# A hybrid decoder layer in three-word fp32: Newton steps of three norms on VectorE one step behind, the first gate and up pair seeded in PSUM, residual loads moved back

## The chip, the cores and the metric

The kernel runs on one core of a Trainium2 chip. The metric is the device time of one execution in microseconds (us). The engines are called PE (TensorE, the matmuls), PEld (its weight loads), DVE (VectorE), ACT (ScalarE), POOL (GpSimd) and SP (SyncE, which here only issues DMAs).

## What is computed

One layer on 256 rows of 2048 channels, all in float32: a norm, one projection to queries, keys, values and gates, three kinds of causal attention over 16 heads, a branch projection for each kind with its sigmoid gate, an output projection with residual, a second norm, and a gated feed-forward of width 5632 with residual.

```python
h = rmsnorm(x, g_mix)
proj = h @ w_in                     # q, k, v (16 heads of 128) and 3 x 2048 gates
gates = sigmoid(proj[..., 3 * MIX_WIDTH:])
o_a = stick_breaking_attention(q[:4], k[:4], v[:4])
o_b = moba_attention(norm(q[4:10]), norm(k[4:10]), v[4:10], rel_bias)
o_c = dilated_attention(norm(q[10:]), norm(k[10:]), v[10:], rel_bias)
merged = (gates[0] * (flat(o_a) @ w_branch[:512]) + gates[1] * (flat(o_b) @ w_branch[512:1280])
          + gates[2] * (flat(o_c) @ w_branch[1280:]))
x = x + merged @ w_out
h2 = rmsnorm(x, g_ffn)
gu = h2 @ w_gu
return x + (silu(gu[..., :5632]) * gu[..., 5632:]) @ w_down
```

rmsnorm multiplies by the inverse root of the mean square of a row. The kernel applies that factor, `rstd`, only behind the matmuls, as the scale of the copy that takes a sum out of PSUM.

## The kernel before

**Products.** A weight tile of 128x1024 floats (`w_raw` or `g_raw`, 512 KB) is loaded by SP's queue and split on the fly into two words: ACT casts the high word (`w_hi`), DVE subtracts it and gets the low word (`w_lo`), both at line 110. `product` issues three matmuls: high by high (L181), low by high (L182), high by low (L183). Every weight tile thus costs one cast on ACT, one subtraction on DVE and usually twelve matmuls.

**Pairs.** `project_pair` computes two blocks of 512 columns at once. Over the channel chunks in `WC` it needs seven products instead of eight: some weight tiles are first added on DVE (tiles `u`, `g_raw` at L325 and L336), and the sums of the products (X and Y in the PSUM banks named `ps` or `qs`, Z and V in others) are put together afterwards. `form(ps, f, ...)` is one of the seven. In the plain way, snapshots of X and Z (L320) go to SBUF and are added back later on DVE (L390, L392, L406). With `seed=True` X is copied to Y and Z to V inside PSUM (L365, L367) and later products are summed on top. `begin_pair` does a pair's first loads and splits while the pair before still runs. There are two banks for each of the names `ps` and `qs`, so a new pair waits until the sums that were in its banks have been read.

**What goes beside the products.** Norms, attention, transposes and restored sums are written as generators in two queues, `stages` and `slow_stages`. At each split `advance` takes one step from `stages` (to the next `yield`), and at every other split one from `slow_stages`. How many yields stand between two pieces of work therefore sets how many splits apart they are. From the program so written a scheduler makes the order of each engine's queue. Each engine works through its queue in that order and never past an instruction that waits.

**The norms.** `rsqrt_mean` takes the mean, gets a first inverse root by Ln and Exp on ACT, and improves it with two Newton steps of four small operations each. It serves the first norm (`first_norm`, on POOL before the change), the norms of queries and keys (`rows_to_columns`) and `second_norm`, on DVE. `rstd` is needed by ACT's copy of the first values (`keep_v`, L781), by the gates (L767), and by `keep_qk` (L809, a DVE operation on tile `sst`). The first values are summed in two `ps` banks, the first gate in two `qs` banks; the first pair of queries and keys comes next and has X in the same `ps` banks.

**Attention.** `stick_breaking` masks its matrix `p` on POOL (L554) and yields three times before it multiplies by the values (L647). `softmax_pair` transposes (L203) and multiplies in the same manner.

**Second norm.** `next_h_now` turns the last two chunks of the second norm's input by transposes (chunks 2 and 3) while the first gate and up pair has begun; `second_norm` follows.

**Down projection.** `down_pair` runs twice, over 1024 columns each. In its loop over the plain weight tiles, `seven` supplies the seven products of each chunk in `WD`, with tiles `b11`, `b12`, `b22`, `b21`; the load of `b21` of the first such chunk is pinned in the queue (L107). `take_x1` loads the residual in four pieces of 256 KB (`sc<-x`, also L107), one at each step of the loop from i = 10 on. Meanwhile ACT still turns the last block of the hidden layer with two DMA transposes (L702).

Of the kernel before, what the change touches and what calls it, by code (L numbers as in the profile page):

```python
# [13 lines left out]
ALU = mybir.AluOpType  # L14
# [5 lines left out]
D = 2048  # L20
S = 256
NT = S // P
KT = D // P
HD = 128
# [3 lines left out]
D_FF = 5632  # L28
NF = D_FF // P
NB = 512  # L30
EPS = 1e-6
# [26 lines left out]
def hybrid_block(ctx: ExitStack, tc: tile.TileContext, x, rel_bias, w_in, w_branch, w_out, w_gu, w_down, xT, gains,  # L58
                 onehot, extra, out):
    nc = tc.nc  # L60
# [121 lines left out]
        nc.tensor.matmul(ps, ah, wl, start=False, stop=False, **how)  # L182
        nc.tensor.matmul(ps, al, wh, start=False, stop=stop, **how)  # L183

    def rsqrt_mean(dst, ss, n, cols, engine=nc.vector):

        v = small.tile([P, cols], F32, name=f"rs_v{cols}")
        engine.tensor_scalar(v, ss, 1.0 / n, EPS, op0=ALU.mult, op1=ALU.add)
        y = small.tile([P, cols], F32, name=f"rs_y{cols}")
        nc.scalar.activation(y, v, AF.Ln)  # L190
        nc.scalar.activation(y, y, AF.Exp, scale=-0.5)
        t = small.tile([P, cols], F32, name=f"rs_t{cols}")
        for it in range(2):
            engine.tensor_mul(t, y, y)
            engine.tensor_mul(t, t, v)
            engine.tensor_scalar(t, t, -0.5, 1.5, op0=ALU.mult, op1=ALU.add)
            engine.tensor_mul(dst if it else y, y, t)

    def transpose4(src):

# [236 lines left out]
    rstd = small.tile([P, NT], F32, name="rstd", bufs=1)  # L437
# [70 lines left out]
    def first_norm():  # L508
        for c in range(3, 4):
            squares(rows[c], ss1, c)  # L510
            yield
        sst = small.tile([P, NT], F32, name="sst", bufs=1)
        nc.vector.tensor_reduce(sst, ss1, op=ALU.add, axis=AX.X)
        rsqrt_mean(rstd, sst, D, NT, nc.gpsimd)
        yield

    rest = [rest_of_x()]
# [87 lines left out]
    def stick_breaking(hl, qT, kT, v):  # L605
        z = att.tile([P, 2 * NB], F32, name="att")
        for i in range(2):
            nc.tensor.matmul(z[:, i * S:(i + 1) * S], kT[:, hl + i, 0:P], qT[:, hl + i, :], start=True, stop=True)
        for i in range(2):
            nc.tensor.matmul(z[:, W0 + i * P:W0 + (i + 1) * P], kT[:, hl + i, P:S], qT[:, hl + i, P:S],  # L610
                             start=True, stop=True)
        n = W0 + W1
        l = pa.tile([P, n], F32, name="p", bufs=1)
        nc.scalar.activation(l, z[:, :n], AF.Abs)
        nc.scalar.activation(l, l, AF.Exp, scale=-1.0)
        nc.scalar.activation(l, l, AF.Ln, bias=1.0)
        sp = pa.tile([P, n], F32, name="pT", bufs=1)
        sp_hi = pa.tile([P, n], F32R, name="sp_hi", bufs=1)
        lo = half_kb(F32R), pa.tile([P, W1], F32R, name="sp_lo", bufs=1)
        nc.vector.scalar_tensor_tensor(sp, z[:, :n], 0.0, l, op0=ALU.max, op1=ALU.add)  # L620
        lb = l
        nc.vector.scalar_tensor_tensor(lb, z[:, :n], 0.0, l, op0=ALU.min, op1=ALU.subtract)
        for blk in diag_blocks(sp):
            keep_before(blk)
        nc.scalar.copy(sp_hi, sp)
        for part, cols in zip(lo, (slice(0, W0), slice(W0, n))):
            nc.vector.tensor_sub(part, sp[:, cols], sp_hi[:, cols].bitcast(F32))
        yield
        yield
        yield  # L630
        c = att.tile([P, 2 * NB], F32, name="att")
        late = c[:, 0:W0].rearrange("p (h q) -> p h q", h=2)[:, :, P:S]
        for i, (early, part) in enumerate(((sp_hi[:, 0:W0], sp_hi[:, W0:n]), lo)):
            nc.tensor.matmul(c[:, 0:W0], neg_after, early, start=not i, stop=False, skip_group_check=True)
            nc.tensor.matmul(late, neg_ones, part.rearrange("p (h q) -> p h q", h=2), start=False, stop=bool(i), skip_group_check=True)
            nc.tensor.matmul(c[:, W0:n], neg_after, part, start=not i, stop=bool(i), skip_group_check=True)
        nc.vector.tensor_add(lb, lb, c[:, :n])
        nc.scalar.activation(lb, lb, AF.Exp)
        for blk in diag_blocks(lb):
            keep_before(blk)  # L640
        yield
        yield
        yield
        po = tr.tile([P, 2, S], F32, name="tr")
        for i in range(2):
            cols = slice((hl + i) * HD, (hl + i + 1) * HD)
            nc.tensor.matmul(po[:, i, :], v[:, 0, cols], lb[:, i * S:(i + 1) * S], start=True, stop=False)  # L647
            nc.tensor.matmul(po[:, i, P:S], v[:, 1, cols], lb[:, W0 + i * P:W0 + (i + 1) * P],
                             start=False, stop=True)
        finish(hl, po)  # L650
# [61 lines left out]
    def rows_to_columns(g, sbs, dst):  # L712
        if g:
            ss = pa.tile([P, 4 * NT * 2], F32, name="ss", bufs=1)
            for i, sb in enumerate(sbs):
                junk = half_kb()
                for hd in range(4):
                    cols = slice(hd * HD, (hd + 1) * HD)
                    nc.scalar.activation(
                        junk[:, cols], sb[:, cols], AF.Square, accum_out=ss[:, 4 * i + hd:4 * i + hd + 1])  # L720
                yield
            rr = pa.tile([P, 4 * NT * 2], F32, name="rr", bufs=1)
            rsqrt_mean(rr, ss, HD, 4 * NT * 2)
            yield

        for i, sb in enumerate(sbs):
            if g:
                sb3 = sb.rearrange("p (h d) -> p h d", h=4)
                nc.vector.tensor_mul(sb3, sb3, rr[:, 4 * i:4 * i + 4, None].to_broadcast([P, 4, HD]))
                for _ in range(3):  # L730
                    yield
            j, t = divmod(i, NT)
            pt = transpose4(sb)
            d = dst[j][:, :, t * P:(t + 1) * P]
            if j == 0 and g:
                hs = 4 * g - H_A
                nc.vector.tensor_mul(d, backwards(pt), gq[:, hs:hs + 4, None].to_broadcast([P, 4, P]))
            else:
                nc.scalar.copy(d, pt)
            joined.append(j)  # L740
        yield
# [223 lines left out]
            behind(n + in_at[1] + 1, lambda: h2.put_sums(c, *[r[:, NB:].rearrange("p (k q) -> p k q", k=4) for r in rooms]))  # L965

    def next_h_now(c, xc):
        for _ in range(4 - c):
            yield
        for t in range(NT):  # L970
            pt = transpose4(xc[t])
            hs = half_kb().rearrange("p (k q) -> p k q", k=4)
            nc.vector.tensor_mul(hs, pt, g2[:, 4 * c:4 * c + 4, None].to_broadcast([P, 4, P]))
            h2.put(c, t, hs)
            yield
# [14 lines left out]
    for c in range(4):  # L990
# [13 lines left out]
            h2 = Chunks(pool(h2_stack, "h2p", "left"), "h", KT // 4, WC)  # L1004
            gx = pool(h2_stack, "gx2", "left", 2)
        if c == 3:
            ahead = begin_pair(h2, w_gu, 0, D_FF)
        keep_x1(c, ps, xc)
    pm.close()
    pr = pool(ctx, "pr", "right")  # L1010
# [3 lines left out]
    def second_norm():  # L1014
        sst2 = small.tile([P, NT], F32, name="sst2", bufs=1)
        nc.vector.tensor_reduce(sst2, ss2, op=ALU.add, axis=AX.X)
        rsqrt_mean(rstd2, sst2, D, NT)
        for _ in range(8):
            yield
        tc.keep_in_program_order(nc.scalar.preload_act_table_set("silu_and_others"))  # L1020
        yield
# [82 lines left out]
    def down_pair(c0, mine, spare, queues, more=(), pace=(6, 1)):  # L1104
# [85 lines left out]
        for i, at in enumerate(plain[:-4]):  # L1190
            rest(*at)
            if i >= 4 * len(more):
                next(with_sums, None)
            if i >= 10:
                next(x1_back, None)
            if i >= pace[0]:
                for _ in range(pace[1]):
# [52 lines left out]
```

## Time and profile before

| | |
|---|---|
| median of 3 runs | 1345.14 us (1344.11 to 1345.21) |
| profiled execution | 1351.32 us, span 1349.6 us |
| clock granted to PE, mean | 0.997 |
| PE, PEld busy | 1330.7 (99%), 1152.8 us (85%) |
| DVE, ACT, POOL busy | 1225.7 (91%), 943.3 (70%), 32.8 us (2%) |
| read from HBM | 292.13 MB, 226 GB/s over the span with the writes |

Everything that follows is read from one profiled execution, which is 6.2 us longer than the median of the runs that were timed. Of its 1351.32 us, 1.7 lie around the span. In the rows of the timeline the columns are the start, the duration, the engine, the line, the operation and its tiles; what stands in brackets is how long the engine sat idle before and which engine or load ended that. Durations of neighbours overlap, so what an operation takes in a full queue is the distance from its start to the next one's. By time, the program is: first values and gate to 49 us, queries, keys and attention to about 440, gates to 560, branches to 610, output projection to 690, eleven gate and up pairs to about 1130, and the two down pairs to the end.

### The profile page before, as it was taken

The page shows a single profiled execution, that of the slowest core. Times are in us where ns is not written, and L with a number is a line of the kernel's source. Part 1 is how long each engine was busy: PE and PEld are TensorE (multiplying, and loading weights), DVE is VectorE, ACT ScalarE, POOL GpSimd, SP SyncE. Part 2 cuts the span into 40 slices and gives each one's busy share as a digit, 9 for nine tenths or more (in the row PEclk, how much of TensorE's full clock was granted, in tenths as well). Part 3 has the DMA queues.
Part 4 walks back from the last instruction along what each step waited for, and adds up shares of the span by engine and source line. Part 5 has one row for each costly group of instructions (what it writes and reads, how often), then busy time and mean ns, then how long its engine had stood idle before and what let it go on. Part 6 is the DMA issues. An engine that isn't in the chain of part 4 may idle for free.

```text
span 1349.6 us, 17385 instructions
## 1 busy us (share of the span) xinstructions
PE 1330.7 (99%) x6194; PEld 1152.8 (85%) x6194; DVE 1225.7 (91%) x1294; ACT 943.3 (70%) x1209; POOL 32.8 (2%) x52
## 2 busy tenths in 40 slices
PE   9999999999999999999999999999999999899998
PEld 7788888888888888888878888888888888788887
DVE  6999999999999998784889999999999997899998
ACT  7777778688767666675757778787777786664663
POOL 0301100000000000000000000000000000000000
PEclk9999999999999999999999999999999999899999
DMA  9865556565666757999977767678887788978663
GB/s 342 285 237 171 174 191 226 189 203 171 238 225 239 241 181 227 292 280 221 267 249 246 243 206 243 206 218 262 261 244 256 212 278 222 309 252 276 221 223 103
DMA packets 200407, 314.79 MB, mean 233 GB/s; under 512 B 46424, under 2 KB 58224, under 8 KB 200320
## 3 DMA queue, kind: packets, MB, share of 16 engines
q1 hardware_dynamic: 151632, 291.54, 65.3%
q10 hardware_dynamic: 46800, 16.29, 6.4%
q0 software_dynamic: 1888, 5.86, 1.1%
q8 instruction: 48, 0.79, 0.2%
q14 instruction: 39, 0.32, 0.1%
HBM read 292.13 MB, written 12.60 MB: 226 GB/s over the span
## 4 chain that ended last, share of the span: by engine, by line
PE 43%; DMA 3%; DVE 2%; ACT 1%; issue 1%; SPq 0%; ACTq 0%; DVEq 0%
PE ps L181 4%; PE ps L183 4%; PE ps L182 4%; PE qs L182 4%; PE qs L183 4%; PE qs L181 4%; PE z L181 3%; PE z L182 3%; PE z L183 3%; PE v L181 2%; PE v L183 2%; PE v L182 2%; DVE w_lo L110 1%; PE tr L182 1%; PE tr L183 1%; PE tr L181 1%
## 5 line engine op out<-in xcount | busy, mean ns | idle before, releaser
L110 DVE TENSOR_TENSOR w_lo<-w_raw,w_hi 128x1024 fp32r<-128x1024 f32 x308 | 375.3, 1223 | 69.5 <-ACT w_hi L110 68.5
L110 ACT CAST w_hi<-w_raw 128x1024 fp32r<-128x1024 f32 x308 | 319.7, 1046 | 74.7 <-PE qs L183 18.6
L110 ACT CAST w_hi<-u 128x1024 fp32r<-128x1024 f32 x156 | 162.9, 1048 | 158.7 <-DVE u L325 87.1
L110 ACT CAST w_hi<-g_raw 128x1024 fp32r<-128x1024 f32 x208 | 213.4, 1048 | 75.6 <-DVE g_raw L325 27.4
L110 DVE TENSOR_TENSOR w_lo<-g_raw,w_hi 128x1024 fp32r<-128x1024 f32 x208 | 248.2, 1224 | 7.0 <-ACT w_hi L110 5.5
L110 DVE TENSOR_TENSOR w_lo<-u,w_hi 128x1024 fp32r<-128x1024 f32 x156 | 186.6, 1225 | 11.6 <-ACT w_hi L110 11.1
L182 PE MATMUL ps<-w_lo,h_hi 128*128 128x512 f32 x328 | 125.3, 382 | 1.7 <-DVE w_lo L110 1.6
L183 PE MATMUL ps<-w_hi,h_lo 128*128 128x512 f32 x328 | 124.3, 379 | 0.0
L182 PE MATMUL qs<-w_lo,h_hi 128*128 128x512 f32 x316 | 120.8, 382 | 0.0
L183 PE MATMUL qs<-w_hi,h_lo 128*128 128x512 f32 x316 | 119.9, 379 | 0.0
L181 PE MATMUL ps<-w_hi,h_hi 128*128 128x512 f32 x328 | 117.3, 380 | 0.0
L181 PE MATMUL qs<-w_hi,h_hi 128*128 128x512 f32 x316 | 112.4, 381 | 0.0
L325 DVE TENSOR_TENSOR u<-u,g_raw 128x1024 f32<-128x1024 f32 x88 | 104.3, 1226 | 0.0
L182 PEld LDWEIGHTS ps<-w_lo,h_hi 128*128 128x128 f32 x328 | 62.0, 189 | 11.6 <-DVE w_lo L110 3.1
L181 PEld LDWEIGHTS ps<-w_hi,h_hi 128*128 128x128 f32 x328 | 61.8, 189 | 8.7
L183 PEld LDWEIGHTS ps<-w_hi,h_lo 128*128 128x128 f32 x328 | 62.0, 189 | 8.5
L181 PEld LDWEIGHTS qs<-w_hi,h_hi 128*128 128x128 f32 x316 | 59.6, 189 | 8.7 <-ACT w_hi L110 0.3
L182 PEld LDWEIGHTS qs<-w_lo,h_hi 128*128 128x128 f32 x316 | 59.7, 189 | 8.5 <-issue 0.2
L183 PEld LDWEIGHTS qs<-w_hi,h_lo 128*128 128x128 f32 x316 | 59.7, 189 | 8.3 <-issue 0.2
L336 DVE TENSOR_TENSOR u<-g_raw 128x1024 f32<-128x1024 f32 x44 | 53.8, 1226 | 3.6 <-DMA g_raw<-in_w_gu 3.6
L325 DVE TENSOR_TENSOR g_raw<-g_raw 128x1024 f32<-128x1024 f32 x44 | 51.8, 1222 | 0.0
L181 PE MATMUL v<-w_hi,h_hi 128*128 128x512 f32 x112 | 43.3, 386 | 0.1
(426 smaller groups left out, 2946.4 us busy)
## 6 DMA issues: line engine op xcount, KB each, us to landing
w_raw<-in_w_in SPq DMA_DIRECT2D x100, 512.0 KB, 5.5
g_raw<-in_w_in SPq DMA_DIRECT2D x88, 512.0 KB, 5.3
g_raw<-in_w_gu SPq DMA_DIRECT2D x88, 512.0 KB, 5.5
w_raw<-in_w_gu SPq DMA_DIRECT2D x88, 512.0 KB, 5.7
w_raw<-in_w_down SPq DMA_DIRECT2D x56, 512.0 KB, 5.4
w_raw<-in_w_branch SPq DMA_DIRECT2D x32, 512.0 KB, 5.2
w_raw<-in_w_out SPq DMA_DIRECT2D x32, 512.0 KB, 5.3
g_raw<-in_w_down SPq DMA_DIRECT2D x32, 512.0 KB, 5.8
```

The costliest lines, as they stand in the source:

```text
L110: for op in nc.scalar.copy(hi, src), nc.vector.tensor_sub(lo, src, hi.bitcast(F32)):
L181: nc.tensor.matmul(ps, ah, wh, start=start, stop=False, **how)
L182: nc.tensor.matmul(ps, ah, wl, start=False, stop=False, **how)
L183: nc.tensor.matmul(ps, al, wh, start=False, stop=stop, **how)
L325: tc.keep_in_program_order(nc.vector.tensor_add(d, d, a))
L336: nc.vector.tensor_add(d, a, b)
```

## The change

There are five edits. `rsqrt_mean` becomes a generator that yields once between ACT's first guess and the Newton steps, and the first norm's steps run on DVE instead of POOL. In `stick_breaking` five yields stand ahead of the last products instead of three. The first gate and up pair is seeded, like the ten after it. `next_h_now` yields 7 - 2c times instead of 4 - c times at first (chunk 2: three instead of two; chunk 3: one, as before), and `second_norm` one time less behind its rsqrt, as there is one within it now. In the first down pair the residual loads begin at i = 16 instead of 10.

```diff
@@ -182,19 +182,20 @@
         nc.tensor.matmul(ps, ah, wl, start=False, stop=False, **how)
         nc.tensor.matmul(ps, al, wh, start=False, stop=stop, **how)
 
-    def rsqrt_mean(dst, ss, n, cols, engine=nc.vector):
+    def rsqrt_mean(dst, ss, n, cols):
 
         v = small.tile([P, cols], F32, name=f"rs_v{cols}")
-        engine.tensor_scalar(v, ss, 1.0 / n, EPS, op0=ALU.mult, op1=ALU.add)
+        nc.vector.tensor_scalar(v, ss, 1.0 / n, EPS, op0=ALU.mult, op1=ALU.add)
         y = small.tile([P, cols], F32, name=f"rs_y{cols}")
         nc.scalar.activation(y, v, AF.Ln)
         nc.scalar.activation(y, y, AF.Exp, scale=-0.5)
+        yield
         t = small.tile([P, cols], F32, name=f"rs_t{cols}")
         for it in range(2):
-            engine.tensor_mul(t, y, y)
-            engine.tensor_mul(t, t, v)
-            engine.tensor_scalar(t, t, -0.5, 1.5, op0=ALU.mult, op1=ALU.add)
-            engine.tensor_mul(dst if it else y, y, t)
+            nc.vector.tensor_mul(t, y, y)
+            nc.vector.tensor_mul(t, t, v)
+            nc.vector.tensor_scalar(t, t, -0.5, 1.5, op0=ALU.mult, op1=ALU.add)
+            nc.vector.tensor_mul(dst if it else y, y, t)
 
     def transpose4(src):
...
@@ -511,7 +512,7 @@
             yield
         sst = small.tile([P, NT], F32, name="sst", bufs=1)
         nc.vector.tensor_reduce(sst, ss1, op=ALU.add, axis=AX.X)
-        rsqrt_mean(rstd, sst, D, NT, nc.gpsimd)
+        yield from rsqrt_mean(rstd, sst, D, NT)
         yield
 
     rest = [rest_of_x()]
...
@@ -638,9 +639,8 @@
         nc.scalar.activation(lb, lb, AF.Exp)
         for blk in diag_blocks(lb):
             keep_before(blk)
-        yield
-        yield
-        yield
+        for _ in range(5):
+            yield
         po = tr.tile([P, 2, S], F32, name="tr")
         for i in range(2):
             cols = slice((hl + i) * HD, (hl + i + 1) * HD)
...
@@ -720,7 +720,7 @@
                         junk[:, cols], sb[:, cols], AF.Square, accum_out=ss[:, 4 * i + hd:4 * i + hd + 1])
                 yield
             rr = pa.tile([P, 4 * NT * 2], F32, name="rr", bufs=1)
-            rsqrt_mean(rr, ss, HD, 4 * NT * 2)
+            yield from rsqrt_mean(rr, ss, HD, 4 * NT * 2)
             yield
 
         for i, sb in enumerate(sbs):
...
@@ -965,7 +965,7 @@
             behind(n + in_at[1] + 1, lambda: h2.put_sums(c, *[r[:, NB:].rearrange("p (k q) -> p k q", k=4) for r in rooms]))
 
     def next_h_now(c, xc):
-        for _ in range(4 - c):
+        for _ in range(7 - 2 * c):
             yield
         for t in range(NT):
             pt = transpose4(xc[t])
...
@@ -1004,7 +1004,7 @@
             h2 = Chunks(pool(h2_stack, "h2p", "left"), "h", KT // 4, WC)
             gx = pool(h2_stack, "gx2", "left", 2)
         if c == 3:
-            ahead = begin_pair(h2, w_gu, 0, D_FF)
+            ahead = begin_pair(h2, w_gu, 0, D_FF, True)
         keep_x1(c, ps, xc)
     pm.close()
     pr = pool(ctx, "pr", "right")
...
@@ -1014,8 +1014,8 @@
     def second_norm():
         sst2 = small.tile([P, NT], F32, name="sst2", bufs=1)
         nc.vector.tensor_reduce(sst2, ss2, op=ALU.add, axis=AX.X)
-        rsqrt_mean(rstd2, sst2, D, NT)
-        for _ in range(8):
+        yield from rsqrt_mean(rstd2, sst2, D, NT)
+        for _ in range(7):
             yield
         tc.keep_in_program_order(nc.scalar.preload_act_table_set("silu_and_others"))
         yield
...
@@ -1191,7 +1191,7 @@
             rest(*at)
             if i >= 4 * len(more):
                 next(with_sums, None)
-            if i >= 10:
+            if i >= (10 if more else 16):
                 next(x1_back, None)
             if i >= pace[0]:
                 for _ in range(pace[1]):
```

What it does to the engines' queues is shown at three places. The first is the first norm, at some 43 to 57 us of the trace before. DVE before, from the subtraction that gives the low word of the bias table (`sc`) on; `w_lo` and `b_slo` are low words, `o_raw` holds the sums of the input's chunks:

```order
L229 TENSOR_TENSOR o_raw_97<-o_raw_97 128x2x128
L110 TENSOR_TENSOR sc_475<-sc_473,sc_475 32x12
L809 TENSOR_SCALAR sst_924<-rstd_108 128x2
L110 TENSOR_TENSOR w_lo_565<-g_raw_556,w_hi_564 128x1024
L227 TENSOR_TENSOR o_raw_97<-o_raw_97 128x2x128
L336 TENSOR_TENSOR u_572<-g_raw_556,g_raw_560 128x1024
L110 TENSOR_TENSOR w_lo_569<-g_raw_558,w_hi_568 128x1024
L110 TENSOR_TENSOR b_slo0_101<-o_raw_97,b_shi0_100 128x1024
```

DVE now, the last twelve of the 25 rows from that same subtraction to the first one behind `sst`:

```order
L110 TENSOR_TENSOR w_lo_581<-g_raw_576,w_hi_580 128x1024
L110 TENSOR_TENSOR w_lo_585<-g_raw_578,w_hi_584 128x1024
L195 TENSOR_TENSOR rs_t2_452<-rs_y2_436 128x2
L228 TENSOR_TENSOR o_raw_97<-o_raw_97 128x2x128
L110 TENSOR_TENSOR w_lo_626<-u_572,w_hi_625 128x1024
L196 TENSOR_TENSOR rs_t2_452<-rs_t2_452,rs_v2_434 128x2
L229 TENSOR_TENSOR o_raw_97<-o_raw_97 128x2x128
L197 TENSOR_SCALAR rs_t2_452<-rs_t2_452 128x2
L230 TENSOR_TENSOR o_raw_97<-o_raw_97 128x2x128
L198 TENSOR_TENSOR rstd_108<-rs_y2_436,rs_t2_452 128x2
L809 TENSOR_SCALAR sst_924<-rstd_108 128x2
L110 TENSOR_TENSOR b_slo1_103<-o_raw_97,b_shi1_102 128x1024
```

The second Newton step's four operations (L195 to L198) stand here, between weight splits and the sums of the second chunk of the input (L225 to L230); `rstd` is made behind the last sum. Between the subtraction of `sc` and `rstd` there are now eight operations on 128x1024, four sums on 128x256, L585 and eight small ones.

ACT at the same place before, with `v` the copy of the first values out of the `ps` banks:

```order
L110 CAST w_hi_564<-g_raw_556 128x1024
L781 ACTIVATE v_454<-ps_137,rstd_108 128x512
L781 ACTIVATE v_454<-ps_138,rstd_108 128x512
L110 CAST w_hi_568<-g_raw_558 128x1024
L110 CAST b_shi0_100<-o_raw_97 128x1024
L110 CAST w_hi_580<-g_raw_576 128x1024
L110 CAST w_hi_584<-g_raw_578 128x1024
L767 ACT_TABLE_LOAD
```

ACT now:

```order
L110 CAST w_hi_625<-u_572 128x1024
L110 CAST b_shi1_102<-o_raw_97 128x1024
L781 ACTIVATE v_445<-ps_137,rstd_108 128x512
L781 ACTIVATE v_445<-ps_138,rstd_108 128x512
L767 ACT_TABLE_LOAD
L767 ACTIVATE sc_588<-qs_140,rstd_108 128x512
L767 ACTIVATE sc_591<-qs_139,rstd_108 128x512
L772 ACT_TABLE_LOAD
L110 CAST w_hi_635<-u_573 128x1024
```

The two copies `v` have moved behind six casts, among them `b_shi1`, which needs the sums of the second chunk that stand ahead of `rstd` on DVE. The table load and the sigmoids of the gate follow them directly. On PE, the first matmul into X of the pair (`ps_595`) stood among the last gate matmuls before, and now stands behind all of them.

The second place is the second norm, DVE at some 698 to 707 us of the trace before. Before (L973 and `h_lo3` belong to chunk 3 of the norm's input; `u` and its low words are form 6 of the first gate and up pair):

```order
L973 TENSOR_TENSOR sc_6384<-tr_6379,par_73 128x512
L195 TENSOR_TENSOR rs_t2_6411<-rs_t2_6411,rs_v2_6406 128x2
L196 TENSOR_SCALAR rs_t2_6411<-rs_t2_6411 128x2
L197 TENSOR_TENSOR rstd2_6304<-rs_y2_6408,rs_t2_6411 128x2
L325 TENSOR_TENSOR u_6275<-u_6275,g_raw_6371 128x1024
L325 TENSOR_TENSOR u_6276<-u_6276,g_raw_6373 128x1024
L110 TENSOR_TENSOR h_lo3_5719<-sc_6384,h_hi3_5718 128x4x128
L110 TENSOR_TENSOR w_lo_6435<-u_6275,w_hi_6434 128x1024
L110 TENSOR_TENSOR w_lo_6445<-u_6276,w_hi_6444 128x1024
```

Now:

```order
L326 TENSOR_TENSOR u_6275<-u_6275,g_raw_6369 128x1024
L973 TENSOR_TENSOR sc_6355<-tr_6350,par_73 128x512
L110 TENSOR_TENSOR w_lo_6399<-w_raw_6367,w_hi_6398 128x1024
L195 TENSOR_TENSOR rs_t2_6427<-rs_y2_6406 128x2
L973 TENSOR_TENSOR sc_6382<-tr_6377,par_73 128x512
L326 TENSOR_TENSOR u_6276<-u_6276,g_raw_6371 128x1024
L110 TENSOR_TENSOR w_lo_6424<-u_6275,w_hi_6423 128x1024
L110 TENSOR_TENSOR h_lo3_5719<-sc_6355,h_hi3_5718 128x4x128
L196 TENSOR_TENSOR rs_t2_6427<-rs_t2_6427,rs_v2_6404 128x2
```

The additions for `u` and the first low word of form 6 have moved ahead of `h_lo3` and of seven of the Newton steps' eight operations, and the turned tiles of chunk 3 (L973) stand closer together among them.

The third place is SP's queue in the first down pair, at some 1129 to 1143 us. Before:

```order
L302 DMA w_raw<-in_w_down 128x2x512 x9
L107 DMA sc<-x_93 128x512
L1060 DMA a_raw<-a_mem 128x1024
L302 DMA w_raw<-in_w_down 128x2x512
L107 DMA sc<-x_93 128x512
L107 DMA g_raw<-in_w_down 128x2x512
L302 DMA g_raw<-in_w_down 128x2x512
```

Now:

```order
L303 DMA w_raw<-in_w_down 128x2x512 x9
L1060 DMA a_raw<-a_mem 128x1024
L303 DMA w_raw<-in_w_down 128x2x512
L107 DMA g_raw<-in_w_down 128x2x512
L303 DMA g_raw<-in_w_down 128x2x512
```

Both residual loads ahead of the pinned load of `b21` (L107, `g_raw`) are gone from there; the first of the four now stands nine weight loads and a load of `a_raw` behind it.

## Prediction

> **What bounds the kernel now.** I read the page's busy shares and chain first, then the span cut into stages, then the waits and the engines in order of time in each stage where PE is not full.
>
> ```profile
> PE 1330.7 (99%) x6194; PEld 1152.8 (85%) x6194; DVE 1225.7 (91%) x1294; ACT 943.3 (70%) x1209; POOL 32.8 (2%) x52
> PE 43%; DMA 3%; DVE 2%; ACT 1%; issue 1%; SPq 0%; ACTq 0%; DVEq 0%
> ```
>
> PE is busy for 1330.7 of 1349.6 us, and the chain runs mostly through PE. The change takes no matmul away. So it can only win from the 18.9 us in which PE idles, and from matmuls that run at a lower clock. The stages (columns: window, length, PE, PEld, DVE, ACT, POOL busy, granted clock, DMA share, GB/s):
>
> ```profile
> 50.00:75.00 25.00, 22.81 (x102) 18.60 (x101) 24.24 (x24) 19.89 (x23) 1.69 (x3) 1.00 0.63 190
> 75.00:450.00 375.00, 372.11 (x1797) 324.56 (x1797) 358.77 (x406) 279.58 (x455) 16.36 (x22) 1.00 0.62 208
> 650.00:750.00 100.00, 95.95 (x447) 82.22 (x446) 91.51 (x108) 67.89 (x87) 0.00 (x0) 1.00 0.74 242
> 750.00:1150.00 400.00, 399.90 (x1847) 347.95 (x1846) 377.18 (x352) 300.29 (x332) 0.00 (x0) 1.00 0.79 241
> 1150.00:1160.00 10.00, 6.21 (x19) 4.77 (x18) 7.04 (x8) 6.11 (x7) 0.00 (x0) 0.70 1.04 365
> ```
>
> The idle time sits at four places, and the change touches all four: behind the first norm (2.2 us), in the attention (2.9), at the second norm (4.1), and at 1150 (3.8, with the clock at 0.70 in that row). From 750 to 1150 PE loses 0.1, so nothing can be won there.
>
> **A, the first norm.** Before, the Newton steps run on POOL:
>
> ```profile
> 45.29 0.20 POOL L197 TENSOR_TENSOR rstd<-rs_y,rs_t 128x2 f32<-128x2 f32 x1
> 45.52 1.27 ACT L781 ACTIVATE v<-ps,rstd 128x512 f32<-128x512 f32 x2 [3.47 <-POOL rstd L197]
> 43.22 0.47 DVE L110 TENSOR_TENSOR sc<-sc 32x12 fp32r<-32x12 f32 x1
> 45.52 0.17 DVE L809 TENSOR_SCALAR sst<-rstd 128x2 f32<-128x2 f32 x1 [1.82 <-POOL rstd L197]
> 45.60 1.23 DVE L110 TENSOR_TENSOR w_lo<-g_raw,w_hi 128x1024 fp32r<-128x1024 f32 x1
> 46.74 0.42 DVE L227 TENSOR_TENSOR o_raw<-o_raw 128x256 f32<-128x256 f32 x1
> 47.08 1.22 DVE L336 TENSOR_TENSOR u<-g_raw 128x1024 f32<-128x1024 f32 x1
> 49.32 0.38 PE L183 MATMUL qs<-w_hi,h_lo 128*128 128x512 f32 x1
> 53.68 0.48 PE L182 MATMUL ps<-w_lo,h_hi 128*128 128x512 f32 x1 [1.39 <-DVE w_lo L110]
> ```
>
> rstd is there at 45.5. ACT has waited 3.47 us for it and DVE 1.82, and PE pays 1.39 later, when the low words come late. That looks like a gain for VectorE. But rstd has a third customer: v is the scaled copy out of the first two "ps" banks, and the first pair's X is written into the same banks, so PE may start X only when ACT has read them. Before, that was at 46.7, while PE still had gate matmuls to do (the last starts at 49.32).
>
> In the new order the Newton steps' eight small operations are spread over DVE's queue, which is full. Between the low word of sc and rstd stand eight operations on 128x1024 (45.60 to 46.74: 1.14 each, 9.1), four sums on 128x256 (46.74 to 47.08: 0.34 each, 1.4), L585 (L584 before) and eight small ones. For the rest I need these rows:
>
> ```profile
> 51.95 0.53 DVE L584 TENSOR_TENSOR sc<-sc,tr 12x384 f32<-12x384 f32 x1
> 699.32 0.15 DVE L194 TENSOR_TENSOR rs_t<-rs_y 128x2 f32<-128x2 f32 x1
> 50.59 1.28 ACT L767 ACT_TABLE_LOAD   x1
> 51.89 1.27 ACT L767 ACTIVATE sc<-qs,rstd 128x512 f32<-128x512 f32 x2
> 54.46 1.99 ACT L110 CAST w_hi<-u 128x1024 fp32r<-128x1024 f32 x2
> 65.25 0.38 PE L181 MATMUL ps<-w_hi,b_shi 128*128 128x512 f32 x1
> 65.46 0.38 PE L182 MATMUL ps<-w_lo,b_shi 128*128 128x512 f32 x1
> ```
>
> L585 takes 0.5, a small one at most 0.15 (I take 0.1, since its start is hidden). The low word of sc ends at 43.7, less the 0.34 of one sum that now stands behind it: 43.3 + 9.1 + 1.4 + 0.5 + 0.8 = 55.1 for rstd, instead of 45.5. On ACT the cast b_shi1, which needs the last of those sums, is ahead of v: 55.0 + 0.95 + 0.6 puts the first bank free at 56.6. PE ends its gate matmuls at 49.3, since the one X matmul that filled a slot among them now stands behind. It idles 7.3 us where it idled 1.39.
>
> From there to the row of 65.46 are 61 matmuls at 0.215 (the spacing at full clock, as from 65.25 to 65.46): 69.7. But ACT still has the second v, a table load, two sigmoids and a table load (1.28 + 1.27 + 1.28) ahead of w_hi of the second u, so that cast ends at 62.0; DVE then does three low words and an addition of 1.14 each, with two casts between, the cast of form 6 ends at 68.0, and 13 matmuls later stands that row: 71.0. Cost 5.5. If 7.3 us of idling halves the clock as 3.79 us does in D, PE needs 2.6 us more, of which 1.3 hide in its wait for that cast: 72.3, cost 6.8. I take +6.2, between the ends 5.5 and 6.8, as no row tells them apart. What covered X's wait before, gate matmuls, is used up at 49.3 in both. The POOL waits removed are in this sum.
>
> **B, the attention.** Two more steps between the last masks of stick-breaking and its products; rsqrt in rows_to_columns one step later.
>
> ```profile
> PE ps L182 <- DVE w_lo L110: 1.1, 3, 0.5
> PE tr L203 <- ACT pT L685: 0.6, 1, 0.6
> 147.78 2.00 POOL L554 TENSOR_SCALAR_AFFINE_SELECT p<-p 128x256 f32<-128x256 f32 x2 [9.52 <-issue]
> 148.49 0.70 PE L647 MATMUL tr<-p,v 128*128 128x256 f32 x2 [1.04 <-POOL p L554]
> ```
>
> Two splits later is some 5 us (24 matmuls), against a POOL lateness of 1.04 us: that wait goes. Of the other 1.7 us a part goes, because A makes PE later by more than it makes DVE (w_lo of form 6 some 5 us late, PE 5.5 to 6.8). Ends: all 2.9 idle won, or nothing won and one such wait of 1.0 new. I take -1.7.
>
> **C, the seeded first pair and the second norm.**
>
> ```profile
> 690.60 1.29 DVE L981 TENSOR_TENSOR sc<-ps,sc 128x512 f32<-128x512 f32 x2
> 702.81 0.48 PE L181 MATMUL qs<-w_hi,h_shi 128*128 128x512 f32 x1 [0.74 <-ACT w_hi L110]
> 704.61 0.48 PE L182 MATMUL qs<-w_lo,h_shi 128*128 128x512 f32 x1 [1.31 <-DVE w_lo L110]
> 709.28 2.36 DVE L110 TENSOR_TENSOR w_lo<-g_raw,w_hi 128x1024 fp32r<-128x1024 f32 x2 [0.19 <-ACT w_hi L110]
> ```
>
> DVE limits here. From L981 to form 7's first low word (709.28) it needs 18.7 us. By the new order the same eleven large operations (12.5) and six of 0.6 stand there, but six small ones instead of ten, and form 6 comes ahead of the Newton steps: 16.7 without waits. Since before has waits in it, too, I halve the 2.0: -1.0, and -0.3 for the two snapshots that become copies and two DVE operations that go. Ends: 0, and the 2.05 that PE waits there: -1.3. The copies into PSUM cost ACT what the snapshots did.
>
> **D, the residual loads.** Two loads of 256 KB leave SP's queue ahead of b21's first load (L107, g_raw), the DMAs moved with nothing else:
>
> ```profile
> 1138.08 1.25 ACTq L702 DMA_TRANSPOSE a_lo<-a_lo  x1
> 1138.82 0.57 SPq L107 DMA_DIRECT2D sc<-x  x1
> 1139.44 0.83 SPq L107 DMA_DIRECT2D g_raw<-in_w_down  x1
> 1151.19 0.38 PE L181 MATMUL tr<-w_hi,a_shi 128*128 128x512 f32 x1
> 1152.94 1.23 DVE L1162 TENSOR_TENSOR u<-u,g_raw 128x1024 f32<-128x1024 f32 x1 [5.24 <-DMA g_raw<-in_w_down]
> 1155.36 0.79 PE L182 MATMUL tr<-w_lo,a_shi 128*128 128x512 f32 x1 [3.79 <-DVE w_lo L110]
> 1156.37 0.63 PE L181 MATMUL tr<-w_hi,a_shi 128*128 128x512 f32 x1
> 1156.80 0.63 PE L182 MATMUL tr<-w_lo,a_shi 128*128 128x512 f32 x1
> g_raw<-in_w_down SPq DMA_DIRECT2D x32, 512.0 KB, 5.8
> ```
>
> DVE waits 5.24 for b21 with form 7's low word queued behind, PE waits 3.79, and then twelve matmuls come every 0.43 instead of 0.215: 2.6 more. The load took 13.5 us (1139.44 to 1152.94) instead of 5.8, with two transposes of 256 KB in flight. At the 365 GB/s of the 1150 row a 256 KB load is 0.7: one surely in the way, the other issued 5.5 us earlier, perhaps. So 0.7 to 1.4 sooner; I take -1.0. The transposes, not the residual, stay as cause. Ends: 0, and 3.79 + 2.6 = -6.4. The loads go to where PE doesn't idle, before their sums are due.
>
> [...] The idle of 1.39 at 53.68 left the granted clock at 1.00 in the row of its stage, that of 3.79 took it to 0.70; a gap between the two stands in no row. [...]
>
> **Sum.** 6.2 - 1.7 - 1.3 - 1.0 = +2.2. On the profiled execution (1351.32) that is 1353.5. The timed median, 1345.14, lies 6.2 lower, so I put the 2.2 on it: 1347.3. 0.2% (2.7 us) is what a measurement can tell here.
>
> **Rivals.**
> 1. D brings nothing, and A's clock falls. The 6.2 between profile and median is nearly D's whole loss (6.4): the timed runs may not have that stall. Then 6.8 - 1.7 - 1.3 = +3.8: 1348.9, slower. Against it: one profile does not say which runs stall.
> 2. B wins nothing and one wait of 1.0 comes up at another of its products, whose steps all move: 2.2 + 1.7 + 1.0 = +4.9: 1350.0. Against it: waits are few there.
> 3. D's gap falls below what halves the clock: 2.6 more won, 2.2 - 2.6 = -0.4: 1344.7. For it: 3.79 is the only gap of this size with a lower clock behind it. Against it: D's gap would still be 2.8, nearer to 3.79 than to the 1.39 that cost nothing. [...]
> 4. The other side: b21 lands before form 7's low word is due. PE needs it 3.79 earlier; from there the stall and slow matmuls are gone, -6.4 in place of -1.0: -3.2, 1341.9. Against it: two loads are 1.4 at most.
> 5. A does as its name says: rstd comes early, X isn't held. Then -1.4 in place of +6.2: -5.4, 1339.7. Against it: the queue counted above.
>
> **How the numbers follow.** The forecast 0.36, rivals 0.24, 0.12, 0.12, 0.09, 0.07. Of the forecast's 0.36 I give 0.29 to no change, 0.04 to slower and 0.03 to faster, as its 2.2 is near the upper bound. Faster: that and rivals 4 and 5, 0.19. Slower: that and rivals 1 and 2, 0.40. Same: that and rival 3, 0.41. The range, 1340.8 to 1351.0, leaves out most of rival 5 and cases where several ends meet (all ends high: 6.8 + 1.0 + 0 + 0 = +7.8, 1352.9). The forecast's own range is 1345 to 1349.
>
> **What would show it.** A: rstd near 55, PE idle about 7 us before the first ps matmul of L182 near 49 to 57, clock below 1 behind it, no POOL Newton rows. B: no wait of PE for POOL near 150. C: the form 6 wait near 704 gone, 650 to 750 with about 1 us less idle. D: DVE's wait for g_raw near 1150 about 1 us shorter. It is wrong if rstd comes before 50, if the attention returns PE's delay (then PE was not the bound there), or if D's stall vanishes.

## The result and the profile after

The changed kernel takes 1361.87 us (1360.68 to 1364.42, 4 runs); the kernel before took 1344.62 (1343.38 to 1345.21, 4 runs) beside it. The ratio is 1.0119 with a 95% interval of 1.009 to 1.0147, that is 16.0 us slower (12.1 to 19.8). The forecast was 2.2 slower, and the range ended at 1351.0. In the sessions below the kernel before has medians of 1345.6 to 1346.9, so everything is compared by ratios to it; 0.001 is 1.35 us.

The page after, its first line:

```profile
PE 1336.2 (98%) x6194; PEld 1155.7 (85%) x6194; DVE 1227.5 (90%) x1301; ACT 943.0 (69%) x1209; POOL 23.0 (2%) x43
```

The stages (columns as in the prediction; the two later stages lie about 10 us later than before):

```profile
50.00:75.00 25.00, 19.63 (x81) 16.85 (x82) 18.72 (x24) 15.78 (x18) 1.13 (x2) 0.86 0.48 165
75.00:450.00 375.00, 364.44 (x1736) 315.33 (x1735) 346.95 (x393) 270.36 (x443) 12.02 (x18) 0.99 0.58 196
660.00:760.00 100.00, 98.26 (x457) 84.21 (x456) 89.57 (x107) 68.91 (x88) 0.00 (x0) 1.00 0.82 261
1150.00:1170.00 20.00, 19.95 (x93) 17.17 (x92) 17.63 (x17) 15.02 (x17) 0.00 (x0) 1.00 0.99 253
```

In the stage of the first norm PE idles 5.4 of 25 us, not 2.2, with the clock at 0.86 (its gap begins at 48.6, so another 1.4 us of it lie ahead of this row). In the attention it idles 10.6, not 2.9. At the second norm it idles 1.7, not 4.1, and at 1150 to 1170 nothing is left to speak of. So two stages lost and two won, and the loss that decides is in the attention, where the prediction had a small gain.

The first norm, by engine:

```profile
53.57 0.15 DVE L198 TENSOR_TENSOR rstd<-rs_y,rs_t 128x2 f32<-128x2 f32 x1
53.69 1.04 ACT L110 CAST b_shi<-o_raw 128x1024 fp32r<-128x1024 f32 x1 [3.96 <-DVE o_raw L230]
54.64 1.26 ACT L781 ACTIVATE v<-ps,rstd 128x512 f32<-128x512 f32 x2
55.37 0.80 PE L181 MATMUL ps<-w_hi,h_hi 128*128 128x512 f32 x1 [6.78 <-ACT v L781]
```

rstd comes at 53.6, the cast b_shi behind the last sum, v behind the cast, and PE's first X matmul is released by v after 6.78 us: each step as forecast. Behind it the clock is at half, for eleven matmuls:

```profile
55.20:60.00 4.80, 4.63 (x11) 3.73 (x12) 0.79 (x1) 4.74 (x7) 1.13 (x2) 0.50 0.40 138
```

In the attention PE waits for this (waits of PE from 75 to 450; us in total, times, longest):

```profile
PE ps L181 <- ACT w_hi L110: 3.3, 3, 1.6
PE qs L181 <- ACT w_hi L110: 3.0, 3, 1.5
PE tr L204 <- DVE sc L729: 1.4, 4, 0.8
PE ps L182 <- DVE w_lo L110: 1.3, 3, 0.8
```

None of the first three was there before. They come at three places, where the three groups of heads with a norm are turned. L729 multiplies the queries and keys by rr, the result of their norm; L204 transposes them. DVE at the first place, before:

```profile
153.73 1.22 DVE L110 TENSOR_TENSOR w_lo<-w_raw,w_hi 128x1024 fp32r<-128x1024 f32 x1
154.86 2.35 DVE L325 TENSOR_TENSOR g_raw<-g_raw 128x1024 f32<-128x1024 f32 x2
157.13 0.17 DVE L194 TENSOR_TENSOR rs_t<-rs_y 128x16 f32<-128x16 f32 x1
157.22 1.22 DVE L110 TENSOR_TENSOR w_lo<-g_raw,w_hi 128x1024 fp32r<-128x1024 f32 x1
```

And after, DVE (the dots stand for L196 to L198 and L195 to L197):

```profile
160.00 1.21 DVE L110 TENSOR_TENSOR w_lo<-w_raw,w_hi 128x1024 fp32r<-128x1024 f32 x1
161.13 0.16 DVE L195 TENSOR_TENSOR rs_t<-rs_y 128x16 f32<-128x16 f32 x1
...
162.58 0.17 DVE L198 TENSOR_TENSOR rr<-rs_y,rs_t 128x16 f32<-128x16 f32 x1
162.79 0.69 DVE L729 TENSOR_TENSOR sc<-sc,rr 128x512 f32<-128x512 f32 x1
163.40 2.35 DVE L326 TENSOR_TENSOR g_raw<-g_raw 128x1024 f32<-128x1024 f32 x2
165.67 1.89 DVE L729 TENSOR_TENSOR sc<-sc,rr 128x512 f32<-128x512 f32 x3
```

ACT and PE in the same stretch:

```profile
164.65 2.18 ACT L110 CAST w_hi<-g_raw 128x1024 fp32r<-128x1024 f32 x2 [2.46 <-DVE g_raw L326]
163.57 0.63 PE L204 MATMUL tr<-ident,sc 128*128 128x128 f32 x4
165.75 0.48 PE L181 MATMUL ps<-w_hi,b_shi 128*128 128x512 f32 x1 [1.56 <-ACT w_hi L110]
166.41 0.66 PE L204 MATMUL tr<-ident,sc 128*128 128x128 f32 x4 [0.18 <-DVE sc L729]
167.83 0.70 PE L181 MATMUL qs<-w_hi,h_hi 128*128 128x512 f32 x2 [0.77 <-ACT w_hi L110]
```

Before, the additions for form 7 (g_raw) follow the low word at once, 1.13 us after its start, and the Newton steps come later, one by one between weight splits. After, all eight Newton operations and the first multiplication stand ahead of those additions, 3.4 us after the low word's start. The block of eight stands at the other two places as well. The small operations stand 0.21 apart in it, where each needs the result of the one before; before, where a weight split came next, the split began 0.09 behind (157.13 and 157.22). ACT's high word of form 7 waits for the additions, and PE, with the transposes ahead of it in its queue, waits for both.

### The profile page after: what moved, and what is told of

Same layout as the page of the kernel before. It is cut to its first block, busy times and chain, and to the rows that moved or that the text cites. A ratio compares the mean times of both kernels' runs of the same rounds, so it can differ in the third digit from the quotient of the medians.

```text
span 1360.4 us, 17383 instructions
## 1 busy us (share of the span) xinstructions
PE 1336.2 (98%) x6194; PEld 1155.7 (85%) x6194; DVE 1227.5 (90%) x1301; ACT 943.0 (69%) x1209; POOL 23.0 (2%) x43
## 4 chain that ended last, share of the span: by engine, by line
PE 78%; DVE 7%; ACT 6%; DMA 5%; issue 3%; SPq 0%; ACTq 0%; DVEq 0%
PE ps L181 10%; PE ps L182 10%; PE ps L183 10%; PE qs L182 9%; PE qs L181 9%; PE qs L183 8%; PE z L182 4%; PE z L181 4%; PE z L183 4%; ACT w_hi L110 3%; DVE w_lo L110 3%; PE v L181 2%; PE v L183 2%; PE v L182 2%; PE tr L182 1%
## 5 line engine op out<-in xcount | busy, mean ns | idle before, releaser
L181 PE MATMUL ps<-w_hi,h_hi 128*128 128x512 f32 x328 | 120.3, 386 | 7.5 <-ACT v L781 6.8
```

What stands on the lines that cost most here:

```text
L181: nc.tensor.matmul(ps, ah, wh, start=start, stop=False, **how)
```

## The experiments

Sixteen kernels ran. The first four undo parts of the change in the changed kernel, where `rsqrt_mean` has its engine back as an argument and yields only `if behind`.

**Query and key norms without the yield.**

```diff
-            yield from rsqrt_mean(rr, ss, HD, 4 * NT * 2)
+            yield from rsqrt_mean(rr, ss, HD, 4 * NT * 2, behind=False)
```

> The changed kernel with one thing undone: in rows_to_columns the Newton steps of the query and key norms follow the first guess in the same step again. Theory 1 (that one yield makes the scheduler put the eight Newton operations and the first multiplication by rr in one block ahead of form 7's addition, so form 7's words come late and PE idles at 157-168, 254-257 and 304-308): the attention loses 2 to 4 us as before instead of about 10.6, the time falls by 8 to 11 us to about 1352. Theory 2 (the five yields of stick-breaking shift the attention's pieces into these places): no more than 2 us less, 1360. Theory 3 (PE's late start at the first norm puts PE and DVE out of step in the whole attention): 1360 to 1362.

Measured: ratio 1.0038 (1.002 to 1.0056), 10.9 us less than the changed kernel. (A difference of two such ratios carries the noise of both, here 4 to 5 us either way.) PE's waits in the attention:

```profile
PE ps L182 <- DVE w_lo L110: 2.3, 4, 0.8
PE qs L181 <- ACT sc L813: 0.7, 1, 0.7
PE tr L205 <- ACT pT L686: 0.6, 1, 0.6
```

The waits for form 7's high word and for the multiplications are gone. Theory 1 holds.

**First norm on POOL.**

```diff
-        yield from rsqrt_mean(rstd, sst, D, NT)
+        yield from rsqrt_mean(rstd, sst, D, NT, nc.gpsimd, False)
```

> The changed kernel with the first norm's Newton steps on POOL again, without the yield there. Theory 1: only the first norm's own loss goes, PE idle before X from 6.8 to about 1.4 us and the eleven slow matmuls behind it, 6 to 7.5 us, to about 1355; the three places in the attention stay as they are. Theory 2: the same, 1355. Theory 3 (late start puts the attention out of step): the attention's loss goes too, 15 us, to about 1346.

Measured: 1.0074 (1.005 to 1.0097), 6.1 us less. The attention keeps its loss:

```profile
75.00:450.00 375.00, 364.00 (x1726) 314.37 (x1725) 346.38 (x392) 269.66 (x441) 12.04 (x18) 0.99 0.58 199
```

So theory 3, that PE's late start spoils the attention, falls.

**Three yields in stick-breaking** (`range(5)` to `range(3)`).

> The changed kernel with three yields in stick-breaking instead of five. Theory 1: little moves, between -1 and +2 us (the wait of PE for POOL of about 1 us comes back), 1361 to 1364; the three places stay. Theory 2 (the five yields are the attention's loss): 8 to 11 us less, 1352. Theory 3: no change, 1362.

Measured: 1.0114 (1.0094 to 1.0134), no change. Theory 2 falls.

**Both undone.**

> The changed kernel with both undone: first norm on POOL without the yield, and query and key norms without the yield. What is left of the change is the five yields, the seeded first pair with the second norm's delays, and the residual loads. Theory 1: both losses are gone and add up, 1362 - 7 - 10 = 1345, less the gain at the second norm of about 2: 1342 to 1345, the same as before or a little faster. Theory 2: 1354. Theory 3: 1344 to 1346.

Measured: 0.9983 (0.9967 to 0.9999), 18.3 less than the changed kernel, and a little faster than before: the two causes are all of the loss.

The next ones add parts to the kernel before.

**The yield in the query and key norms alone.**

```diff
-            rsqrt_mean(rr, ss, HD, 4 * NT * 2)
+            yield from rsqrt_mean(rr, ss, HD, 4 * NT * 2)
```

> The kernel before with one thing added: the yield between first guess and Newton steps in the query and key norms only. Theory 1 (that yield alone is the attention's loss): slower by 8 to 12 us, 1354 to 1358, with blocks of eight Newton operations at three places and PE idle there. Theory 2 (it needs the rest of the change, such as stick-breaking's later products or PE's late start): within 3 us of before.

Measured: 1.0053 (1.0035 to 1.0071), 7.1 slower. It needs nothing else of the change, but costs less than the forecast of 8 to 12. In its attention stage PE idles 9.8 us, 6.9 more than before:

```profile
75.00:450.00 375.00, 365.21 (x1745) 315.65 (x1745) 350.04 (x396) 272.03 (x444) 14.21 (x18) 1.00 0.59 201
```

**Second norm's part alone** (`begin_pair(..., True)`, `7 - 2 * c`, second norm's Newton steps one step behind).

> The kernel before with the second norm's part alone: first gate and up pair seeded, next_h_now 7 - 2c, Newton steps of the second norm one step behind. The working of the prediction: 1 to 2 us faster, 1343 to 1344. What the runs without the query and key yield show (PE not idle at all from 660 to 760): up to 5.5 us faster, 1340.

Measured: 0.9962 (0.994 to 0.9984), 5.1 faster (2.2 to 8.1). From 650 to 750:

```profile
650.00:750.00 100.00, 99.95 (x471) 87.04 (x471) 93.97 (x110) 69.80 (x88) 0.00 (x0) 1.00 0.76 243
```

**Residual loads alone** (`if i >= 16`).

> The kernel before with the residual loads of the first down pair from i = 16 alone. The prediction's term: DVE's wait for b21's load near 1150 about 1 us shorter, with a stall of PE of 2.8 left: 1344 to 1345. Rival 1 (the timed runs do not have this stall): no change, 1345 to 1346, though the profile may show the wait gone. Rival 4: wait gone and 6 us faster, 1339.

Measured: 0.9983 (0.9966 to 1.0): between nothing and 4.6 faster, so the run alone doesn't tell the theories apart. The profiles of all kernels do better. In the eight of them with these loads at i = 10, DVE's wait for b21 is 0.5 to 5.2 us; in the ten with i = 16 it is 0 to 1.4. The lowest with i = 10 (DVE's waits in the kernel with the query and key yield; us in total, times, longest):

```profile
DVE u L1163 <- DMA g_raw<-in_w_down: 0.5, 1, 0.5
```

the highest, in the kernel before:

```profile
DVE u L1162 <- DMA g_raw<-in_w_down: 5.2, 1, 5.2
```

and the highest with i = 16, in the kernel that comes next:

```profile
DVE u L1163 <- DMA g_raw<-in_w_down: 1.4, 1, 1.4
```

The PE wait that follows from it is 0 to 3.8 with i = 10 and none with i = 16. The profile that the prediction was read from was the worst of the eight.

**The parts that win, and the cast off POOL.** Second norm's part and residual loads on the kernel before, and

```diff
-        nc.gpsimd.tensor_copy(oh_r[:N_BUCKETS, :NDIST], oh_sb[:N_BUCKETS, :NDIST])
+        nc.scalar.copy(oh_r[:N_BUCKETS, :NDIST], oh_sb[:N_BUCKETS, :NDIST])
```

> The kernel before with the second norm's part and the residual loads, three yields in stick-breaking, first norm on POOL, and the cast of the one-hot table (L579, on POOL between the first norm's steps before) on ACT instead, so that nothing stands between the Newton steps on POOL. If rstd's lateness behind that cast costs PE its 1.4 us at 53 us, this is 1 to 2 us faster than the kernel with both yields undone (1342.4): 1340 to 1341. If not, 1342.

Measured: 0.9943 (0.9926 to 0.9961), 7.7 faster than before; 1339.27 (1338.09 to 1341.02). It beats both kernels.

**Nobody waits for rstd.** In the changed kernel, first values and, in the same way, first gate with scale 1.

```diff
-  nc.scalar.activation(v[:, t, :], ps[t], AF.Copy, scale=rstd[:, t:t + 1])
+  nc.scalar.activation(v[:, t, :], ps[t], AF.Copy, scale=rstd[:, t:t + 1] if g else 1.0)
```

> The changed kernel in which the copy of the first values and the first gate's sigmoid leave the factor rstd out (scale 1 instead; those two results are then not the reference's). The Newton steps stay on DVE and rstd comes as late as before, near 55 us, but nothing reads it in time. If the step 'X waits for the banks that v's copy, waiting for rstd, holds' is right: PE's idle of 6.8 us and the slow matmuls behind it go, 5 to 7 us, to about 1355 to 1357, like undoing the first norm's move. If instead DVE's load by the nine small operations delays the weights' low words: no change, 1361.

Measured: 1.0057 (1.0035 to 1.0078), 8.3 less than the changed kernel. rstd comes no earlier (55.8), and the wait of 6.78 is gone; the largest near it is

```profile
55.78 0.15 DVE L198 TENSOR_TENSOR rstd<-rs_y,rs_t 128x2 f32<-128x2 f32 x1
57.05 0.48 PE L181 MATMUL qs<-w_hi,b_shi 128*128 128x512 f32 x1 [1.40 <-ACT b_shi L110]
```

So it is the readers of rstd, not the work added to DVE. The edit frees the gate's sigmoid as well as v; that it is v and its banks for which PE waits is in the row of 55.37 above.

**One step behind, with no step more.** In the changed kernel:

```diff
             yield from rsqrt_mean(rr, ss, HD, 4 * NT * 2)
-            yield
```

> The changed kernel with all norms' Newton steps one step behind as it has them, but with the next yield of rows_to_columns taken away, so that the multiplications by rr and the transposes stand at the split where they stood before. If the delay of these (the additional step) is what costs and not the Newton steps' being behind: as fast as the kernel without the yield, 1348 to 1352. If the Newton steps' later place is what costs: 1360 to 1362.

Measured: 1.0015 (0.9999 to 1.003), as fast as without the inner yield (1.0038, 1.002 to 1.0056). The order of every engine's instructions is the same in these two, one by one: they are one order measured twice, and by the second the additional step costs 14.0 in the changed kernel where the first gave 10.9. So it isn't the Newton steps' place in the program that costs, but the additional step, which puts the multiplications and transposes one split later.

**Five yields alone.**

> The kernel before with five yields in stick-breaking alone. The prediction's term (POOL's wait of 1 us goes, the rest absorbed): 1 to 2 us faster, 1344. What the profiles of the runs with and without it show (150 to 200 us: 2.8 of loss with five, 0.8 with three): 1 to 3 us slower, 1348.

Measured: 1.0002 (0.9982 to 1.0021). No change: the interval, 2.4 faster to 2.8 slower, holds a part of both forecasts and doesn't tell them apart.

**Seeding alone.**

> The kernel before with the seeded first pair alone, next_h_now and second_norm as before. If the seeding brings what the second norm's part brought (1346.9 to 1341.3): 1341 to 1342. If the delays of next_h_now and the Newton steps bring it: 1345 to 1346.

Measured: 0.9996 (0.9976 to 1.0015). The seeding by itself brings nothing that shows.

The single values (first norm 6.1, query and key norms 7.1, second norm -5.1, loads -2.3) add up to 5.8 of the 16.0. Four more runs were made for this.

**First norm alone on the kernel before** (`yield from rsqrt_mean(rstd, sst, D, NT)`).

> The kernel before with the first norm's Newton steps on DVE, one step behind, alone. The prediction's term: 5.5 to 6.8 us slower, 1351 to 1352.5. If PE's delay is partly returned in the attention when that is otherwise as before: 3 to 5 us slower.

Measured: 1.0042 (1.0021 to 1.0063), 5.6 slower. The attention returns nothing of it: its stage reads 371.83 of 375 busy, as against 372.11.

```profile
75.00:450.00 375.00, 371.83 (x1795) 324.26 (x1794) 357.84 (x404) 279.30 (x454) 13.31 (x19) 1.00 0.61 204
```

**Both causes, nothing else.**

> The kernel before with both causes, first norm on DVE and the additional step in the query and key norms, and nothing else of the change. If they add: 6 + 7 = 13 us slower, 1358 to 1359. If they make each other dearer: 16 to 18 us, 1361 to 1363, and then the gains of the rest of the change are worth nothing in the changed kernel.

Measured: 1.014 (1.0105 to 1.0174), 18.8 slower (14.1 to 23.4), where the two alone make 12.7. The interval of the pair allows both, but with the rest of the change at -2.3 (both undone) the account closes within that noise: 18.8 - 2.3 = 16.5, against 16.0.

**Second norm's part and residual loads alone.**

> The kernel before with the second norm's part and the residual loads: the changed kernel with first norm, query and key norms and stick-breaking's yields undone. If the five yields ate the gain: -7 us, 1338 to 1340. If the cast on ACT made the difference: -2 to -4 us, 1342 to 1344.

Measured: 0.9968 (0.9947 to 0.9989), 4.3 faster. Between this and 2.3 with five yields, the intervals overlap.

**The cast alone.**

> The kernel before with the cast of the one-hot table on ACT instead of POOL, alone. If rstd's lateness behind that cast costs PE its idle time near 53 us: 1 to 2 us faster. If not: no change.

Measured: 0.9989 (0.9964 to 1.0015). Not settled. That 7.7 is the sum of 4.3 and a small gain here would fit all intervals; it isn't shown.

## Why the prediction was wrong

**A, the first norm: right.** Forecast 6.2 with ends 5.5 and 6.8; measured 5.6 alone, 6.1 undone, and 8.3 where nobody reads rstd. rstd at 53.6 (55.1 forecast), PE idle for 6.78 (7.3), then eleven matmuls at half the clock (0.50), as in the upper end. The rival that the change does what it says fell by the queue counted from the order, as argued. That the order of a full queue, not the speed of an operation, sets when a result is there, was read from the order alone and held.

**B, the attention: here it failed.** The step is the clause "rsqrt in rows_to_columns one step later". It was named and given no price; all of B's -1.7 was worked out for stick-breaking, which turned out to move nothing that shows (1.0002, 0.9982 to 1.0021). The additional step, by which the multiplications and transposes come a split later, costs 7.1 alone and 10.9 to 14.0 in the changed kernel. In the profile of the changed kernel that is 7.7 us more of PE's idle time in the attention and two stretches at a lower clock, 1.7 each (last section). The rows for a price were there. DVE was nearly full in that stage (358.8 of 375 us), four multiplications (0.6 each) and eight dependent operations (0.21 each) make 4.1 us a place, and there are three places: 12 if all of it is in the way of form 7; in the new order the eight and one multiplication are (3.4 less 1.13 us at the first place, so some 7 for three). The new order shows the block of eight at these three places; the prediction reads it at the first norm, the second norm and the down pair, and not there. Rival 2 had the right place and sign, "one wait at another of its products", but the wrong part of the change and 1.0 where it needed 10. The prediction's sign for B, no wait of PE for POOL near 150, came true: a sign that watches only for the gain does not show a new loss.

**C, the second norm: sign right, size open.** Forecast -1.3, ends 0 and -2.05; measured -5.1 (-2.2 to -8.1) alone, so too small by that run, but -4.3 with the loads, which alone measured -2.3. I had bounded the gain by two waits of form 6, where the whole stage's 4.05 was the bound. PE's idle time there is 0.1 in the profile of the part alone, but that is no measure of the part: the kernel with the residual loads alone, which leaves this stage as it was, idles 0.7.

```profile
650.00:750.00 100.00, 99.28 (x467) 86.38 (x466) 94.40 (x112) 69.33 (x87) 0.00 (x0) 1.00 0.72 239
```

Over the eight kernels without the second norm's delays it is 0.7 to 4.1 in this window, over the ten with them 0 to 2.4, so the profile that the prediction was read from was the worst of the eight here, too. Seeding alone gave nothing that shows, so the delays or both together give the gain; which, wasn't tried. Even one order gives different values: two kernels whose order is the same in every row, those without the additional step, had 0.0 and 2.3 us of PE idle time from 650 to 750 in their profiles. The kernel with the inner yield taken away:

```profile
650.00:750.00 100.00, 100.00 (x473) 87.39 (x472) 91.11 (x109) 67.85 (x87) 0.00 (x0) 1.00 0.77 245
```

and the one with the next yield taken away, in which ACT waits there for loads of w_out, as it does not in the other:

```profile
ACT w_hi L110 <- DMA w_raw<-in_w_out: 7.7, 4, 3.1
```

```profile
650.00:750.00 100.00, 97.69 (x454) 83.52 (x453) 89.29 (x107) 67.99 (x87) 0.00 (x0) 1.00 0.78 256
```

**D, the residual loads: right in kind, too small in the profile.** Forecast -1.0; measured -2.3 (-4.6 to 0). The profile after has the stall gone, which the prediction named as a sign of being wrong and gave to rival 4, where the forecast left 2.8 of it:

```profile
1155.54 0.59 SPq L107 DMA_DIRECT2D g_raw<-in_w_down  x1
1166.11 1.23 DVE L1162 TENSOR_TENSOR u<-u,g_raw 128x1024 f32<-128x1024 f32 x1 [0.86 <-DMA g_raw<-in_w_down]
```

The load took 10.6 us, not 13.5, where 0.7 to 1.4 less was forecast. But in five of the kernels with i = 10 the same load took 8.7 to 13.5, so one pair of profiles doesn't size this term. "The transposes, not the residual, stay as cause" was half right: 10.6 is still far above the median of 5.8, but DVE hardly waits for it. The suspicion that most timed runs don't have the stall of 3.8 is supported: the other seven kernels with the same loads have 0 to 2.3, and of the 101 timed executions of the kernel before, 20 have a mean granted clock of 0.997 or less, as the profiled one has, at 1349.7 us on average; the 39 at 1.000 take 1343.7.

**What stays open.** Why the scheduler puts the Newton steps in one block as soon as the multiplications stand one split later; and why the additional step costs more in other company than its 7.1 alone, if it does. It isn't the late first norm: in the changed kernel the step costs 12.2 with the first norm on POOL (1.0074 against 0.9983) and 10.9 to 14.0 with it on DVE; added to the kernel before with the first norm on DVE, it costs 13.2 (1.014 against 1.0042). Part of it is the clock: between the two kernels of the 12.2 the mean granted clock of the timed executions falls from 0.9998 to 0.9965, which is 4.5 us; with the step alone it doesn't fall (0.9987 and 0.9986). What is left lies within the noise of the differences.

## What to carry to other kernels

Where a generator's yields set the distance between pieces of work, a yield more moves everything behind it, in every place that uses the function: count the steps, and read the new order at each of these places, not only where the change is meant to act. A late result costs what its last reader holds: here a copy out of PSUM held the banks of the next product, and PE idled 6.78 us for it, which no wait in the profile before showed. One profiled execution can be the worst of eight, here at two places; a stall that depends on a DMA's landing (8.7 to 13.5 us for the same load here) needs a second look before it is priced.

## What the runs showed of the hardware

The clock fell without a long idle time. At the second and third place in the attention of the changed kernel, PE idled at most 1.5 us at a time, yet the clock was 0.62 and 0.69 right behind it; at the first place it stayed at 1.00 (last two rows):

```profile
253.00:257.50 4.50, 2.47 (x14) 1.57 (x12) 4.50 (x7) 3.42 (x4) 0.00 (x0) 1.00 0.13 51
257.50:262.00 4.50, 4.50 (x17) 3.80 (x16) 4.50 (x5) 2.13 (x4) 0.00 (x0) 0.62 0.00 0
304.00:308.50 4.50, 1.74 (x9) 1.02 (x9) 4.50 (x7) 2.75 (x3) 0.00 (x0) 1.00 0.00 2
308.50:314.00 5.50, 5.17 (x18) 4.39 (x19) 5.50 (x7) 3.13 (x5) 0.00 (x0) 0.69 0.01 3
163.60:168.00 4.40, 1.90 (x11) 1.13 (x11) 4.40 (x6) 3.26 (x4) 0.00 (x0) 1.00 0.16 61
168.00:175.00 7.00, 7.00 (x39) 6.17 (x40) 7.00 (x8) 5.82 (x8) 0.00 (x0) 1.00 0.24 61
```

What PE did at all three for some 4 us was eight transposes and a matmul or two with gaps between. So a gap's length alone, which the prediction reasoned with, doesn't tell: the longest was 1.08 at the second place and 1.49 at the third, where the clock fell, and 1.56 at the first, where it didn't. Nor does PE's busy share, since it is 2.47 of 4.5 and 1.74 of 4.5 where the clock fell and lies between, 1.90 of 4.4, where it didn't. Both falls cost the same: 4.5 us at 0.62 and 5.5 at 0.69 are 1.7 us lost each, as much as 3.4 us at half the clock would lose (in the first of the two the matmuls of 260.46, 260.88 and 261.31 start 0.43 apart, those from 261.55 on 0.22). Why the clock fell behind two of the places and not behind the other isn't shown: no run here took the transposes away. In the kernel with the query and key yield alone, and in the one with both causes and nothing else, the clock was 1.00 around the first two places and 0.85 from 300 to 310, around the third. PE idles 11.0 us in the attention both in the changed kernel with the first norm on POOL and in the one where nobody waits for rstd; the clock of that stage was 0.99 in the first and 1.00 in the second.

The cast L579 on POOL took 3.71 us in the kernel before. In the kernel with both causes undone it took 1.49 at the same place in POOL's queue; why isn't known:

```profile
39.96 3.71 POOL L579 CAST sc<-sc 32x384 fp32r<-32x384 f32 x1
```

```profile
37.51 1.49 POOL L581 CAST sc<-sc 32x384 fp32r<-32x384 f32 x1
```
